# Making three rows' second products in one GpSimd instruction, in a buffer of its own, in a rotary-embedding kernel

## The chip, the cores and the metric

The kernel runs on one core of a Trainium2 chip. The metric is the device time of one execution in microseconds (us). Before the change it was 162.52 us, the median of 3 runs (162.47 to 162.65). A profile of one execution accompanies each kernel; its span, from the first instruction to the last, is 1.8 to 2.0 us shorter than the time.

## The reference

```python
batch, seq, dim = (16, 512, 1024); num_heads = 16      # head_dim 64, half_dim 32, all float32
x = x.reshape(batch, seq, num_heads, head_dim)
x1, x2 = x[..., :half_dim], x[..., half_dim:]
cos, sin = cos[None, :, None, :], sin[None, :, None, :]
out = concatenate([x1 * cos - x2 * sin, x1 * sin + x2 * cos], axis=-1)
```

Each element is one product with a cosine, one product of its partner in the other half of the head with a signed sine, and a sum. 32 MB are read and 32 MB written.

## The kernel before

The data go through in eight tiles of 4 MB. A tile has 128 partitions with 8 rows of 1024 elements each. GpSimd makes the second (sine) products of rows 1 to 7 into buffers `b`. VectorE (DVE) makes the cosine products into PSUM, the memory into which TensorE also adds. For the pairs (1, 2), (4, 5) and (6, 7) DVE also makes the sum. Row 3 goes half by half through one PSUM bank, `pe_ps`: DVE puts the cosine product there, TensorE adds `b` to it (a matmul with the identity), and ScalarE copies it out. Row 0 does without GpSimd.

```python
PAIRS = ((1, 2), (4, 5), (6, 7))
bp = ctx.enter_context(tc.tile_pool(name="bp", bufs=3))     # three buffers of 8 KB per partition
...
def sin_rows(t, k, n):                                     # GpSimd: n rows from row k
    b = bp.tile([P, 2 * dim], FP32, name="b")[:, : n * dim]
    sin_product(b, rows(t, k, n), k, n)
    return b
def pe_half(k, r, b):
    cos_product(pe_ps, r, k)                               # DVE
    pe_add(pe_ps, b)                                       # TensorE
    nc.scalar.copy(out=r, in_=pe_ps)                       # ScalarE
...
for t in range(NT):
    first, second, third = PAIRS
    b1 = sin_rows(t, first[0], 2)
    p1 = pair_product(t, first[0])                         # DVE
    ...                                                    # row 0: DVE, TensorE, ScalarE
    b3 = sin_rows(t, ROW_PE, 1)
    b2 = sin_rows(t, second[0], 2)
    pair_sum(*p1, b1)                                      # DVE
    h0, h1 = zip(parts(rows(t, ROW_PE)), parts(b3))
    pe_half(ROW_PE, *h0)
    p2 = pair_product(t, second[0])
    b1 = sin_rows(t, third[0], 2)
    pair_sum(*p2, b2)
    pe_half(ROW_PE, *h1)
    p1 = pair_product(t, third[0])
    if t + 1 < NT:
        cos_product(own_ps, rows(t + 1, ROW_OWN), ROW_OWN)
    pair_sum(*p1, b1)
    stores(t)
```

## Time and profile before

| | before |
|---|---|
| time, median | 162.52 us |
| span of the profile | 160.7 us |
| busy: DVE, GpSimd, TensorE, ScalarE | 136.3, 127.2, 56.4, 18.1 us |
| last store: issued, landed | 148.15, 159.84 us |

### The profile page before, as it was taken

Reading aid. Unit: us, or ns where it says so; the run is one execution under the profiler, and the core shown is the slowest. Engines: PE = TensorE matmul, PEld = TensorE weight load, DVE = VectorE, ACT = ScalarE, POOL = GpSimd, SP = SyncE. Lnnn points to the kernel's source line nnn. Section 1 sums busy time; section 2 is a strip of 40 time slices with the busy share of each in tenths; the row PEclk is TensorE's granted clock in tenths of the full one; section 3 lists DMA queues with packets and bytes.
Section 4 is the critical chain, followed back from the end, with each engine's and each line's share of the span. In section 5 each row is a group of like instructions: output and inputs, shape, how many; then the busy total and the mean of one; then the engine's idle time right before and its main releaser. Section 6 shows DMA issues by size and latency. Waiting matters only on the chain.

```text
span 160.7 us, 443 instructions
## 1 busy us (share of the span) xinstructions
PE 56.4 (35%) x71; PEld 18.8 (12%) x71; DVE 136.3 (85%) x85; ACT 18.1 (11%) x25; POOL 127.2 (79%) x38
## 2 busy tenths in 40 slices
PE   3131905064503731191309150745046402822000
PEld 0111301021102210121004010211021101210000
DVE  1059969999999999999999999999999999998000
ACT  0001311003000301021100310031003010201000
POOL 1049999999999999988998899898999899840000
PEclk9999985559555865567555855595558655675555
DMA  5999999999999999999999999999999999999993
GB/s 180 407 408 473 392 498 416 392 457 457 392 416 481 408 400 498 408 392 506 410 392 473 432 400 449 457 400 416 489 392 408 498 400 408 481 416 400 392 514 139
DMA packets 2619, 67.25 MB, mean 419 GB/s; under 512 B 314, under 2 KB 442, under 8 KB 442
## 3 DMA queue, kind: packets, MB, share of 16 engines
q1 hardware_dynamic: 2618, 67.24, 97.9%
q14 instruction: 1, 0.01, 0.0%
HBM read 33.69 MB, written 33.55 MB: 418 GB/s over the span
## 4 chain that ended last, share of the span: by engine, by line
DVE 68%; issue 12%; POOL 6%; DMA 4%; PE 1%; SPq 0%; DVEq 0%
DVE xt L189 33%; DVE pd L141 31%; POOL b L165 6%; DMA b<-in_sin_dram 4%; DVE pe_ps L141 3%; PE tab L113 1%; PE tab L114 1%; DVE sns L116 0%; DVE xt L150 0%; DVE own_ps L141 0%; SPq L74 0%; DVE sns L117 0%; DVEq L189 0%
## 5 line engine op out<-in xcount | busy, mean ns | idle before, releaser
L165 POOL TENSOR_TENSOR b<-xt,sns 128x2048 f32<-128x2048 f32 (+1 forms) x32 | 126.5, 3987 | 14.5 <-DVE sns L117 9.1
L189 DVE TENSOR_TENSOR xt<-pd,b 128x2048 f32<-128x2048 f32 x24 | 54.9, 2287 | 2.4 <-POOL b L165 1.6
L141 DVE TENSOR_TENSOR pd<-xt,tab 128x2048 f32<-128x2048 f32 x24 | 55.0, 2291 | 0.2
L176 PE MATMUL own_ps<-xt,ident 128*128 128x512 f32 x32 | 29.1, 1064 | 54.0 <-DVE xt L150 48.3
L176 PE MATMUL pe_ps<-b,ident 128*128 128x512 f32 x32 | 25.2, 880 | 29.1 <-DVE pe_ps L141 29.1
L176 PEld LDWEIGHTS own_ps<-xt,ident 128*128 128x128 f32 x32 | 9.4, 324 | 74.0 <-DVE xt L150 59.3
L209 ACT COPY xt<-own_ps 128x1024 f32<-128x1024 f32 x8 | 8.1, 1013 | 72.2 <-PE own_ps L176 72.2
L181 ACT COPY xt<-pe_ps 128x512 f32<-128x512 f32 x16 | 9.4, 589 | 40.7 <-PE pe_ps L176 40.7
L176 PEld LDWEIGHTS pe_ps<-b,ident 128*128 128x128 f32 x32 | 8.0, 279 | 43.8 <-DVE pe_ps L141 36.0
L141 DVE TENSOR_TENSOR pe_ps<-xt,tab 128x512 f32<-128x512 f32 x16 | 11.0, 686 | 0.0
L141 DVE TENSOR_TENSOR own_ps<-xt,tab 128x1024 f32<-128x1024 f32 x8 | 9.8, 1223 | 0.0
L150 DVE TENSOR_TENSOR xt<-xt,tab 128x1024 f32<-128x1024 f32 x8 | 9.7, 1214 | 0.0
L116 DVE TENSOR_SCALAR sns<-tab 128x256 f32<-128x256 f32 x1 | 0.4, 426 | 8.0 <-PE tab L114 8.0
L209 ACT ACT_TABLE_LOAD x1 | 1.3, 1283 | 15.3 <-DVE xt L150 15.3
L113 PE MATMUL tab<-b,spread 64*128 64x256 f32 x2 | 1.2, 697 | 4.9 <-DMA b<-in_sin_dram 4.9
L101 PE MATMUL own_ps<-zero 128*128 128x512 bf16 x2 | 1.0, 622 | 1.2 <-DVE zero L97 1.2
L113 PEld LDWEIGHTS tab<-b,spread 64*128 64x128 f32 x2 | 0.5, 308 | 5.7 <-issue 5.7
L114 PE MATMUL tab<-b,spread 64*128 64x256 f32 x2 | 1.1, 631 | 0.0
L97 DVE MEMSET zero<- 128x256 uint32 x1 | 0.3, 272 | 0.9 <-PEq L240 0.9
L114 PEld LDWEIGHTS tab<-b,spread 64*128 64x128 f32 x2 | 0.7, 333 | 0.2
L101 PE MATMUL pe_ps<-zero 128*128 128x512 bf16 x1 | 0.6, 634 | 0.0
L101 PEld LDWEIGHTS <-zero 128*128 128x128 bf16 x3 | 0.3, 125 | 1.5 <-DVE zero L97 1.2
(9 smaller groups left out, 1.8 us busy)
## 6 DMA issues: line engine op xcount, KB each, us to landing
out_dram<-xt SPq DMA_DIRECT2D x8, 4096.0 KB, 21.4
xt<-in_x_dram SPq DMA_DIRECT2D x7, 4096.0 KB, 38.8
xt<-in_x_dram SPq DMA_DIRECT2D x1, 2560.0 KB
xt<-in_x_dram SPq DMA_DIRECT2D x1, 1536.0 KB
spare<-in_sin_dram SPq DMA_DIRECT2D x5, 0.1 KB
b<-in_sin_dram SPq DMA_DIRECT2D x1, 64.0 KB
b<-in_cos_dram SPq DMA_DIRECT2D x1, 64.0 KB
```

The lines of the kernel that those rows point to most:

```text
L97: nc.vector.memset(zero, 0.0)
L101: nc.tensor.matmul(out=ps, lhsT=zero[:, :P], rhs=zero, start=True, stop=True)
L113: nc.tensor.matmul(out=sin_t, lhsT=spread, rhs=sin_sb, start=True, stop=True)
L114: nc.tensor.matmul(out=cos_t, lhsT=spread, rhs=cos_sb, start=True, stop=True)
L116: nc.vector.tensor_scalar_mul(out=sns[:, :, 0, :], in0=sin_k, scalar1=-1.0)
L141: nc.vector.tensor_tensor(out=o, in0=i, in1=cb, op=ALU.mult)
L150: nc.vector.tensor_tensor(out=heads(r), in0=heads(r), in1=s, op=ALU.mult)
L165: nc.gpsimd.tensor_tensor(out=o, in0=i, in1=sb, op=ALU.mult)
L176: nc.tensor.matmul(out=ps, lhsT=ident, rhs=other, start=False, stop=True, skip_group_check=True)
L181: nc.scalar.copy(out=r, in_=pe_ps)
L189: nc.vector.tensor_tensor(out=r, in0=ps, in1=b, op=ALU.add)
L209: nc.scalar.copy(out=r0, in_=own_ps)
```

## The change

The intent is fewer GpSimd instructions: rows 3, 4 and 5 lie side by side, so their second products can be one instruction. Its result needs 12 KB per partition. One of three 8 KB buffers is given up for it, and two small early tiles, `zero` and `spread`, are laid into the new buffer; together that frees 9.5 of the 12 KB. Seven no-ops are put on GpSimd ahead of its first wait.

```diff
+GROUPS = ((1, 2), (3, 3), (6, 2))
-    bp = ctx.enter_context(tc.tile_pool(name="bp", bufs=3))
+    bp = ctx.enter_context(tc.tile_pool(name="bp", bufs=2))
+    bp3 = ctx.enter_context(tc.tile_pool(name="bp3", bufs=1))
...
-    zero = fixed.tile([P, BANK], BF16)
+    for _ in range(7):
+        nc.gpsimd.nop(hint="pause")
+    early = bp3.tile([P, 3 * dim], FP32, name="b3")
+    zero = early[:, : BANK // 2].bitcast(BF16)
-    spread = fixed.tile([PB, P], FP32)
+    spread = early[:PB, BANK : BANK + P]
...
-        b3 = sin_rows(t, ROW_PE, 1)
-        b2 = sin_rows(t, second[0], 2)
+        b2 = sin_rows(t, *GROUPS[1])
         pair_sum(*p1, b1)
-        h0, h1 = zip(parts(rows(t, ROW_PE)), parts(b3))
+        h0, h1 = zip(parts(rows(t, ROW_PE)), parts(b2[:, :dim]))
...
-        pair_sum(*p2, b2)
+        pair_sum(*p2, b2[:, dim:])
```

More of the change, by code (lines that the diff above doesn't have):

```diff
@@ L167, in sin_rows @@
     def sin_rows(t, k, n):
-        b = bp.tile([P, 2 * dim], FP32, name="b")[:, : n * dim]
+        b = bp.tile([P, 2 * dim], FP32, name="b") if n == 2 else bp3.tile([P, 3 * dim], FP32, name="b3")
         sin_product(b, rows(t, k, n), k, n)
@@ L202 @@
         first, second, third = PAIRS
-        b1 = sin_rows(t, first[0], 2)
+        b1 = sin_rows(t, *GROUPS[0])
         p1 = pair_product(t, first[0])
@@ L209 @@
         nc.scalar.copy(out=r0, in_=own_ps)
-        b3 = sin_rows(t, ROW_PE, 1)
-        b2 = sin_rows(t, second[0], 2)
+        b2 = sin_rows(t, *GROUPS[1])
         pair_sum(*p1, b1)
-        h0, h1 = zip(parts(rows(t, ROW_PE)), parts(b3))
+        h0, h1 = zip(parts(rows(t, ROW_PE)), parts(b2[:, :dim]))
         pe_half(ROW_PE, *h0)
         p2 = pair_product(t, second[0])
-        b1 = sin_rows(t, third[0], 2)
-        pair_sum(*p2, b2)
+        b1 = sin_rows(t, *GROUPS[2])
+        pair_sum(*p2, b2[:, dim:])
         pe_half(ROW_PE, *h1)
```

## The prediction

> **What bounds the kernel now.** I read the page first: its busy shares, then the DMA row, then the chain that ended last.
>
> ```profile
> PE 56.4 (35%) x71; PEld 18.8 (12%) x71; DVE 136.3 (85%) x85; ACT 18.1 (11%) x25; POOL 127.2 (79%) x38
> DMA  5999999999999999999999999999999999999993
> q1 hardware_dynamic: 2618, 67.24, 97.9%
> HBM read 33.69 MB, written 33.55 MB: 418 GB/s over the span
> ```
>
> Two things are nearly full at once. The DMA queue moves 67.24 MB and its packets fill 97.9% of 16 engines' span of 160.7 us. VectorE is busy for 85% of the span, but between the first tile and the last it doesn't stop: cut into stretches of one tile (16.98 us), the view by windows shows this.
>
> ```profile
> 64.95:81.93 16.98, 6.50 (x8) 2.15 (x8) 16.84 (x11) 2.09 (x3) 15.84 (x5) 0.60 1.00 433
> 81.93:98.91 16.98, 6.55 (x8) 2.15 (x8) 16.84 (x11) 2.09 (x3) 15.85 (x5) 0.60 1.00 432
> ```
>
> The pairs are busy us and count for PE, PEld, DVE, ACT, POOL, then PEclk, DMA share and GB/s. DVE fills 16.84 of 16.98 us, GpSimd only 15.84; the DMA share is 1.00. So in the steady state DVE sets the pace of the computing, GpSimd has 1.14 us to spare per tile, and the transfers run through without a hole.
>
> The groups and the waits say where an instruction of GpSimd ever holds up DVE:
>
> ```profile
> L165 POOL TENSOR_TENSOR b<-xt,sns 128x2048 f32<-128x2048 f32 x24 | 108.4, 4530 | 14.5 <-DVE sns L117 9.1 <-DVE xt L189 5.4
> L165 POOL TENSOR_TENSOR b<-xt,sns 128x1024 f32<-128x1024 f32 x8 | 18.9, 2360 | 0.0
> L189 DVE TENSOR_TENSOR xt<-pd,b 128x2048 f32<-128x2048 f32 x24 | 54.9, 2287 | 2.4 <-POOL b L165 1.6
> ```
>
> DVE's sums (L189) lose 1.6 us to GpSimd in the whole run, in one wait: the timeline has it in tile 0 at 21.78 us, where the second pair's product is late because GpSimd could not start before 10.44 us. After tile 2 it is the other way round: GpSimd waits for DVE's sums to free a buffer (5.4 us, ten times).
>
> What ends the run is the last store. The trace has it issued at 148.15 us, right after DVE's last sum (145.80 + 2.29 = 148.09), and landed at 159.84. Whether it starts on idle or still busy DMA engines is seen in narrow windows around it (only the DMA columns count here):
>
> ```profile
> 148.55:148.95 0.40, 0.00 (x0) 0.00 (x0) 0.00 (x0) 0.00 (x0) 0.00 (x0) 0.50 0.20 82
> 148.95:149.35 0.40, 0.00 (x0) 0.00 (x0) 0.00 (x0) 0.00 (x0) 0.00 (x0) 0.50 2.87 1229
> 149.35:149.75 0.40, 0.00 (x0) 0.00 (x0) 0.00 (x0) 0.00 (x0) 0.00 (x0) 0.50 0.00 0
> 149.75:150.15 0.40, 0.00 (x0) 0.00 (x0) 0.00 (x0) 0.00 (x0) 0.00 (x0) 0.50 0.19 82
> 158.00:158.50 0.50, 0.00 (x0) 0.00 (x0) 0.00 (x0) 0.00 (x0) 0.00 (x0) 0.50 0.15 66
> 158.50:159.60 1.10, 0.00 (x0) 0.00 (x0) 0.00 (x0) 0.00 (x0) 0.00 (x0) 0.50 0.01 0
> ```
>
> Bytes count where a packet starts, and a packet has 32 KB. 82 GB/s over 0.40 us is one packet; 1229 is fifteen. So fifteen engines begin the last store at 148.95 to 149.35, some 0.8 us after its issue, while one engine started a packet of the store before at 148.6 (its packets take 1.2 us) and begins the last store only at 149.8. In the packets' own records the fifteen end at 158.7 to 159.0 and that one at 159.51. It never idles. **The end is thus the late DMA engine's, and DVE's last sum has a slack of about 159.51 - 159.0 = 0.5 us in front of it.**
>
> **What the Trainium skill says.** (1) "SBUF — State Buffer", Who interferes with whom: a DVE instruction with two SBUF inputs contends with a GpSimd instruction that reads SBUF, one with a single SBUF input doesn't. All the large DVE instructions here take one input from PSUM, and the trace agrees: the sum takes 2.29 us beside GpSimd and also at 145.80, when GpSimd is through. So a longer GpSimd instruction slows DVE by nothing. (2) "GPSIMD Engine Reference", Elementwise, side by side: 4497 ns for a tensor_tensor of 2048 f32; the trace has 4530. (3) "PSUM — Partial Sum Buffer", Engine vs sequencer instructions: a nop is executed by the sequencer alone, not by the datapath. The kernel before has none, so no row shows a cost. (4) "DMA: Bandwidth & Descriptors", Why a DMA increments its semaphore by 16: the 16 engines finish independently and only the full count means landed. That is the late engine above.
>
> **The change part by part.**
> *Products.* Per tile GpSimd made 2 rows + 1 row + 2 rows + 2 rows; now 2 + 3 + 2. From the two groups a row costs 4530 - 2360 = 2170 ns and an instruction 2360 - 2170 = 190 ns beside. A 3-row product is estimated at 190 + 3 x 2170 = 6.70 us, against 2.36 + 4.53 = 6.89. But the trace starts the next instruction some 0.05 us before the last ends (14.91 + 2.36 = 17.27, next start 17.22), so the gain is about 0.15 us per tile, 1.2 us over 8 tiles, of GpSimd's time. GpSimd is off the path after tile 0, so there it is worth nothing.
>
> *Tile 0, the second pair.* Before: 14.91 start of row 3, end of rows 4 and 5 near 21.74, sum at 21.78. After: 14.91 + 6.70 = 21.61, sum at about 21.64. DVE gains 0.14 us.
>
> *Tile 0, row 3.* Row 3's product was ready at 17.27; now it comes with the rest at 21.61. TensorE adds it into pe_ps, ScalarE copies it out, and only then can DVE put the second half's cos product into pe_ps. Before, TensorE's addition ran at 18.85 for 1.44 us and ScalarE's copy ended at 20.91, long before DVE came by at 23.99. Now: 21.65 + 1.44 (or 2.08, the same work at half clock at 24.73) + 0.06 + 0.59 + 0.03 = 23.8 to 24.4. DVE's sum would let it go on at 21.64 + 2.21 = 23.85. So DVE goes on at 23.85 to 24.4 instead of 23.99: a shift between **-0.14 and +0.45 us**, middle +0.15. The wait on b moves, partly, to a wait on ScalarE. As DVE has no hole after it, this shift is carried unchanged to the last sum.
>
> *Buffers.* Counting from the start of the second sum of a tile: the sum ends at 2.29, the second half's cos product at 2.9, TensorE's last reading of the 12 KB buffer at about 2.9 + 2.1 = 5.0. From there GpSimd makes the next 3-row product by 5.0 + 6.7 = 11.7. DVE fills its first half of pe_ps at 14.6 - 0.6 = 14.0 and takes the second sum at 16.98. So at the fastest GpSimd is 2.3 us ahead even of row 3's need and 5.3 ahead of the sum. The third pair follows by 16.2 (needed at 6.14 + 16.98 = 23.1), the next tile's first by 20.7 (needed at 28.8); then GpSimd waits until 22.0, which is some 1.3 us per tile of a wait in place of the two of 0.47 and 0.67 us it has now. No DVE wait. In tile 1, where GpSimd isn't ahead yet, the 3-row product ends at 21.6 + 2 x 4.47 + 6.7 = 37.2 (now the second pair's ends near 37.5); TensorE and ScalarE are through by 37.2 + 2.1 + 0.7 = 40.0, DVE comes at 40.96. Free by 0.9 us.
>
> *No-ops and the early tiles.* The seven no-ops come before GpSimd's wait of 9.1 us for the tables: they would have to cost 1.2 us each to show. zero and spread in the 12 KB buffer save 1.5 KB so that 28 KB of buffers fit in place of 24; their readers are through at about 10 us, well before the 3-row product at 14.91. Nothing.
>
> *Sum.* The last store is issued at 148.15 + (-0.14 to +0.45); its fifteen engines end at 159.0 + the same, up to 159.45, below the late engine's 159.51. Expected: 0.0 to 0.1 us. **162.6 us.**
>
> **The rivals.** *A: the shift comes through.* If the late engine is less late in the new kernel (its lag was not planned, as far as the page shows), the time follows DVE: between -0.5 (no late engine, shift -0.14) and +0.45. For: one engine out of 16 late by 0.5 us is a small thing. Against: before's three times agree within 0.18 us. 162.0 to 163.0. *B: the single 12 KB buffer becomes the bound.* A chain of sum, cos product, TensorE, product through one buffer: 11.7 us against a period of 16.98. It would need TensorE to come 2.3 us later than the throttled 2.08 us; then 8 tiles at some tenths: 163 to 165. Against it the spare time above. *C: GpSimd becomes the bound*, if a product over three rows costs more per element than over two; it would need 15.84 + 1.14: the 3-row product at over 7.9 us instead of 6.70. 1024 and 2048 elements lie on one straight line with a small intercept, which speaks against. *D: a gain*: the 1.57 us of DVE's wait in tile 0 doesn't go away, because all five rows are still made before the second sum; and anything gained there is stopped by 67.24 MB in the DMA queue.
>
> **Range and chances.** The middle is before plus 0.1; rival A gives -0.5 to +0.45, with the spread of runs of 0.2: 162.0 to 163.2 for 8 in 10. 2% is 3.25 us; the gain isn't there to be had (the DMA is full), the loss needs B or C. Faster 0.01, same 0.97, slower 0.02.
>
> **What would show it.** Right: 3-row products at 6.7 us, eight; DVE's wait on b in tile 0 near 1.4 us, with a wait of 0 to 0.5 us on ScalarE's copy after it; GpSimd's waits once a tile, on TensorE; period 16.98; last store issued at 148.0 to 148.6, landing near 159.8. Wrong: DVE waits on b or on ScalarE in several tiles, a period above 17.0, a 3-row product over 7 us, or a hole in the DMA row.

## The result, and the profile after

The changed kernel took 162.52 us, the median of 4 runs (162.47 to 162.64), beside 162.50 us for before. The ratio is 1.0004 with a 95% interval of 0.9987 to 1.0021: the same. (A ratio is the mean time of one kernel's fast runs over that of the other's of the same rounds, so it isn't quite the ratio of the medians quoted.) All runs were fast: none was over 1.5% above the fastest of its kernel.

| | before | after |
|---|---|---|
| time, median | 162.52 us | 162.52 us |
| GpSimd products, first start | 32, 10.44 us | 24, 10.70 us |
| GpSimd busy | 127.2 us | 125.7 us |
| last store: issued, landed | 148.15, 159.84 us | 148.83, 159.91 us |

The total stood still, but not all below it did. First four lines of the view of the groups with shapes kept apart, for the changed kernel (busy us, mean ns, then idle time before and its cause):

```profile
L171 POOL TENSOR_TENSOR b<-xt,sns 128x2048 f32<-128x2048 f32 x16 | 72.2, 4531 | 11.9 <-DVE sns L123 9.4 <-DMA xt<-in_x_dram 2.5
L195 DVE TENSOR_TENSOR xt<-pd,b 128x2048 f32<-128x2048 f32 x24 | 54.9, 2287 | 2.3 <-POOL b L171 1.4
L171 POOL TENSOR_TENSOR b<-xt,sns 128x3072 f32<-128x3072 f32 x8 | 53.5, 6693 | 2.4 <-PE pe_ps L182 2.4
L147 DVE TENSOR_TENSOR pe_ps<-xt,tab 128x512 f32<-128x512 f32 x16 | 11.0, 687 | 0.5 <-ACT xt L187 0.5
```

The three-row product takes 6.69 us. DVE's wait for GpSimd shrank from 1.6 to 1.4 us, and a new one of 0.5 us stands on row 3's cosine product, for ScalarE. GpSimd now waits for TensorE, which reads the 12 KB buffer last.

Where the new wait is, is seen in the timeline of tile 0. First before (start, duration, engine and line; the idle time of the engine before it in brackets):

```profile
18.85 1.44 PE L176 MATMUL pe_ps<-b,ident 128*128 128x512 f32 x2
...
20.32 0.59 ACT L181 COPY xt<-pe_ps 128x512 f32<-128x512 f32 x1 [0.22 <-PE pe_ps L176]
21.78 2.29 DVE L189 TENSOR_TENSOR xt<-pd,b 128x2048 f32<-128x2048 f32 x1 [1.57 <-POOL b L165]
...
23.99 0.69 DVE L141 TENSOR_TENSOR pe_ps<-xt,tab 128x512 f32<-128x512 f32 x1
```

Then after:

```profile
21.90 2.29 DVE L195 TENSOR_TENSOR xt<-pd,b 128x2048 f32<-128x2048 f32 x1 [1.44 <-POOL b L171]
...
21.92 2.07 PE L182 MATMUL pe_ps<-b,ident 128*128 128x512 f32 x2 [2.61 <-POOL b L171]
24.03 0.59 ACT L187 COPY xt<-pe_ps 128x512 f32<-128x512 f32 x1 [3.67 <-PE pe_ps L182]
24.65 0.70 DVE L147 TENSOR_TENSOR pe_ps<-xt,tab 128x512 f32<-128x512 f32 x1 [0.46 <-ACT xt L187]
```

Row 3's product is no longer ready at about 17 us but comes with rows 4 and 5 at 21.9 us. TensorE, ScalarE and DVE then follow one another. DVE goes on at 24.65 instead of 23.99 us, and since it waits for nothing afterwards (the period is 16.98 us as before), the last store is issued 0.68 us later. Of this, 0.26 us was there already when GpSimd began.

Yet the store landed only 0.07 us later. Three windows around the last store of the changed kernel (the last two columns are the DMA share and GB/s, counted where a packet starts):

```profile
148.95:149.35 0.40, 0.00 (x0) 0.00 (x0) 0.00 (x0) 0.00 (x0) 0.00 (x0) 0.50 0.01 0
149.35:149.60 0.25, 0.00 (x0) 0.00 (x0) 0.00 (x0) 0.00 (x0) 0.00 (x0) 0.50 0.00 0
149.60:150.00 0.40, 0.00 (x0) 0.00 (x0) 0.00 (x0) 0.00 (x0) 0.00 (x0) 0.50 3.05 1311
```

1311 GB/s over 0.40 us is sixteen packets of 32 KB: all sixteen engines begin the last store together, where before fifteen began at 149 us and the late one at 149.8. The later issue fell into time in which the late engine was still at work on the store before.

### The profile page after: what moved, and what is told of

It reads as the page before. It is cut to its first block, busy times and chain, and to the rows that moved or that the text cites. A ratio compares the mean times of both kernels' runs of the same rounds, so it can differ in the third digit from the quotient of the medians.

```text
span 160.7 us, 443 instructions
## 1 busy us (share of the span) xinstructions
PE 57.6 (36%) x71; PEld 18.7 (12%) x71; DVE 136.4 (85%) x85; ACT 18.1 (11%) x25; POOL 125.7 (78%) x30
## 4 chain that ended last, share of the span: by engine, by line
DVE 55%; POOL 19%; issue 8%; PE 6%; DMA 4%; ACT 0%; SPq 0%; DVEq 0%; POOLq 0%
DVE xt L195 27%; DVE pd L147 22%; POOL b L171 19%; PE pe_ps L182 5%; DVE pe_ps L147 4%; DMA b<-in_sin_dram 4%; PE tab L119 1%; PE tab L120 1%; ACT xt L187 0%; DVE sns L122 0%; SPq L77 0%; DVE sns L123 0%; DVE xt L156 0%; DVE own_ps L147 0%; DVEq L195 0%
## 5 line engine op out<-in xcount | busy, mean ns | idle before, releaser
L171 POOL TENSOR_TENSOR b<-xt,sns 128x2048 f32<-128x2048 f32 (+1 forms) x24 | 125.0, 5252 | 14.3 <-DVE sns L123 9.4
L182 PE MATMUL pe_ps<-b,ident 128*128 128x512 f32 x32 | 25.9, 904 | 28.3 <-DVE pe_ps L147 25.7
L119 PE MATMUL tab<-b,b 64*128 64x256 f32 x2 | 1.2, 696 | 5.1 <-DMA b<-in_sin_dram 5.1
L107 PE MATMUL own_ps<-b 128*128 128x512 bf16 x2 | 1.0, 622 | 1.2 <-DVE b L103 1.2
L119 PEld LDWEIGHTS tab<-b,b 64*128 64x128 f32 x2 | 0.5, 307 | 6.0 <-issue 6.0
L120 PE MATMUL tab<-b,b 64*128 64x256 f32 x2 | 1.1, 631 | 0.0
L120 PEld LDWEIGHTS tab<-b,b 64*128 64x128 f32 x2 | 0.7, 333 | 0.2
L107 PE MATMUL pe_ps<-b 128*128 128x512 bf16 x1 | 0.6, 634 | 0.0
```

The lines of the kernel that those rows point to most:

```text
L107: nc.tensor.matmul(out=ps, lhsT=zero[:, :P], rhs=zero, start=True, stop=True)
L119: nc.tensor.matmul(out=sin_t, lhsT=spread, rhs=sin_sb, start=True, stop=True)
L120: nc.tensor.matmul(out=cos_t, lhsT=spread, rhs=cos_sb, start=True, stop=True)
L171: nc.gpsimd.tensor_tensor(out=o, in0=i, in1=sb, op=ALU.mult)
L182: nc.tensor.matmul(out=ps, lhsT=ident, rhs=other, start=False, stop=True, skip_group_check=True)
```

## The experiments

Names beginning with `b_` are built on before, those with `a_` on the changed kernel. The "issue" is the start of the last store, "landing" the landing of it, both from the profiled execution. To make differences visible that the slack hides, the five kernels with `d22` in their names make one cosine product of a pair twice in tile 2. This changes no value and moved DVE's next tile 2.3 us later. b_d11 doubles a product of half that size. Every kernel gave correct results.

| kernel | first product | issue | landing | landing - issue | time, median (before beside it) |
|---|---|---|---|---|---|
| before | 10.44 | 148.15 | 159.84 | 11.69 | 162.52 |
| after | 10.70 | 148.83 | 159.91 | 11.08 | 162.52 (162.50) |
| a_again | 10.83 | 148.39 | 160.34 | 11.95 | 162.64 (162.46) |
| b_lead | 10.91 | 147.39 | 160.18 | 12.79 | 162.57 (162.37) |
| a_nonop | 10.55 | 148.12 | 159.82 | 11.70 | 162.50 (162.37) |
| b_d11 | 10.65 | 149.62 | 160.71 | 11.09 | 163.25 (162.37) |
| b_d22 | 10.39 | 150.45 | 161.54 | 11.09 | 164.22 (162.46) |
| a_t0_d22 | 10.45 | 150.49 | 161.57 | 11.08 | 164.56 (162.46) |
| a_d22 | 10.79 | 151.23 | 162.31 | 11.08 | 164.46 (162.46) |
| a_d22b | 10.42 | 150.85 | 161.92 | 11.07 | 164.59 (162.36) |
| a_fill_d22 | 10.39 | 150.29 | 161.37 | 11.08 | 164.08 (162.36) |
| b_2buf | 11.27 | 168.56 | 179.63 | 11.07 | 181.72 (162.37) |

### How much slack the last store has: b_d22 and b_d11

```diff
 # b_d22
         p1 = pair_product(t, third[0])
+        if t == 2:
+            cos_product(p1[0], p1[1], third[0], 2)
 # b_d11
             cos_product(own_ps, rows(t + 1, ROW_OWN), ROW_OWN)
+            if t == 2:
+                cos_product(own_ps, rows(t + 1, ROW_OWN), ROW_OWN)
```

> Before, with one cos product of 128x2048 made twice in tile 2: DVE loses 2.2 us in the steady state. Theory 1 (slack of about 0.6 us, then the time follows the last store's issue one for one: issue + 13.7 us): issue at 150.4, time 164.0 to 164.2, so 1.5 to 1.7 us more than before, not 2.2. Rival (the DMA queue alone is the bound, with much slack): time within 0.3 us of before. Rival (DVE alone is the bound): 2.2 us more.

> Before, with one cos product of 128x1024 made twice in tile 2: DVE loses 1.13 us. Theory 1 (slack about 0.6 us): issue near 149.3, time 0.4 to 0.6 us over before. Rival (DMA bound with wide slack): no more than 0.1 us over. Rival (DVE bound): 1.1 us over.

b_d22 took 164.22 us (164.13 to 164.29), a ratio of 1.0108 (1.0093 to 1.0122). That is 1.76 us more than before: neither nothing nor all of the delay. b_d11 took 163.25 us, ratio 1.0055 (1.0042 to 1.0067), 0.88 us more, which is above the 0.4 to 0.6 expected. The doubled product moved DVE by 1.27 us in the profile, not 1.13, and in the profiled run GpSimd had also begun 0.21 us later. Its issue was therefore 1.47 us later than before's and its landing 0.87. How late the other four runs began isn't recorded, and their times (163.15 to 163.34) are much the same, so some 0.2 us of the 0.88 stays unexplained.

The table's fifth column says the same without any reckoning. A last store that finds the DMA engines idle lands 11.07 to 11.09 us after its issue, in eight profiles (in after's the late engine came free just in time). Before's took 11.69 us. So **its slack was 11.69 - 11.08 = 0.61 us** in this profile, and after's was zero. The times agree roughly: 2.3 - 1.76 = 0.5 us from b_d22, 1.27 - 0.88 = 0.4 from b_d11.

### Does an earlier DVE gain anything: b_lead

In tile 0, rows 4 and 5 come before row 3 on GpSimd, and DVE does row 3's second half after the third pair's cosine product.

```diff
-        b3 = sin_rows(t, ROW_PE, 1)
-        b2 = sin_rows(t, second[0], 2)
+        if t == 0:
+            b2 = sin_rows(t, second[0], 2)
+            b3 = sin_rows(t, ROW_PE, 1)
+        else:
+            b3 = sin_rows(t, ROW_PE, 1)
+            b2 = sin_rows(t, second[0], 2)
...
-        pe_half(ROW_PE, *h1)
+        if t > 0:
+            pe_half(ROW_PE, *h1)
         p1 = pair_product(t, third[0])
+        if t == 0:
+            pe_half(ROW_PE, *h1)
```

> Before, with tile 0 in another order: rows 4 and 5 before row 3 on GpSimd, and on DVE row 3's second half after the third pair's cos product. DVE's wait of 1.6 us in tile 0 goes, the last store is issued 1.0 to 1.6 us earlier, at 146.5 to 147.2. Theory 1 (the DMA engines are full until 149 us and one is late): time unchanged, or up to 0.5 us less if the late engine is less late. Rival (DVE is the bound): 1.0 to 1.6 us less, 161.0 to 161.5.

It took 162.57 us, ratio 1.0014 (1.0002 to 1.0027): nothing gained. The view of the waits of DVE shows the wait for GpSimd almost gone, 0.2 us in place of 1.6:

```profile
DVE xt L189 <- POOL b L165: 0.2, 1, 0.2
```

The last store was issued at 147.39 us although this execution had begun 0.47 us late, and it landed 12.79 us after its issue, at 160.18. The DMA engines were not free earlier. So the kernel before stands on the DMA queue, and DVE may be later by 0.6 us or, as here, earlier by 0.76 + 0.47 = 1.2 us without the time changing.

### The no-ops: a_nonop

```diff
-    for _ in range(7):
-        nc.gpsimd.nop(hint="pause")
```

> The changed kernel without the seven no-ops. Theory: they lie in GpSimd's 9 us of waiting for the tables and take some 0.04 us each, so nothing changes: time within 0.15 us of the changed kernel and of before, GpSimd's first product at 10.4 to 10.7 us. Rival (they steer the fetch of instructions or the late DMA engine): the instruction packet at about 80 us moves or goes, or the time moves by 0.3 us or more.

162.50 us, ratio to before 1.0007 (0.9994 to 1.0021), and the first product at 10.55 us. The one instruction packet in mid-run stays where it was, at 79.8 us. In the changed kernel's trace the seven no-ops have 13 ns each and start 40 ns apart, from 0.98 to 1.22 us; GpSimd is then through with its set-up at 1.3 us and waits until 10.70. They do nothing that these runs show. What they were put in for stays open.

### Is the later issue the change's doing: a_again, a_d22 and a_t0_d22

a_again is the changed kernel once more, a_d22 the changed kernel with the doubled product. a_t0_d22 has, in tile 0 alone, the products apart again:

```diff
+        if t == 0:
+            b2 = bp3.tile([P, 3 * dim], FP32, name="b3")
+            sin_product(b2[:, :dim], rows(t, ROW_PE), ROW_PE, 1)
+            sin_product(b2[:, dim:], rows(t, second[0], 2), second[0], 2)
+        else:
+            b2 = sin_rows(t, *GROUPS[1])
```

> The changed kernel once more, beside before on the same chip. Theory 1 (the change costs DVE about 0.4 us in tile 0, a wait for ScalarE's copy, and the slack in front of the last store swallows it): time within 0.15 us of before, last store issued 0.4 us later than before's, and later still by what the tables happen to land later; DVE's wait for ScalarE 0.4 to 0.5 us, once. Theory 2 (the 0.68 us by which the last store came later was chance in the start alone): the issue varies and the wait for ScalarE is not there in this profile.

> The changed kernel with the same doubled product in tile 2. Theory 1: its slack is used up, so nearly the whole 2.2 us comes through: issue at 150.8 to 151.05, time 164.4 to 164.75, which is 0.4 us more than before with the same delay. Rival (the change shifts DVE by nothing; the later issue was chance): the same time as before with the delay, within 0.15 us.

> The changed kernel with the doubled product in tile 2, and in tile 0 alone the products of row 3 and of rows 4 and 5 made apart again, into the same 12 KB buffer. Theory 1 (what the change costs is the late product of row 3 in tile 0 and nothing else): no wait of DVE for ScalarE, time equal to before with the delay within 0.15 us, 0.4 us under the changed kernel with the delay. Rival (the single buffer or the longer product costs DVE something in later tiles too): it stays at or near the changed kernel's time.

None of the three came out as plainly as expected. a_again took 162.64 us, ratio 1.0012 (0.9998 to 1.0026): the same, but its profile has **no wait for ScalarE**, against my theory 1, and the store was issued only 0.24 us later than before's, less than the 0.39 us by which its first product was late. a_d22 took 164.46 us, inside the expected range, but by luck: its six times fall into two heaps, 164.94, 164.70, 164.82 and 164.06, 163.96, 164.22, with the median between them. Its issue, 151.23 us, lies above the expected range; GpSimd had begun at 10.79. a_t0_d22 took 164.56 us, 0.34 us above b_d22 and no better than a_d22: by the time alone the rival, a cost in later tiles, would have won. The profile speaks against it: no wait for ScalarE, issue 150.49 and landing 161.57 us against b_d22's 150.45 and 161.54. About half of the difference lies outside the span: the time is 1.9 to 2.0 us longer than the span, b_d22's 1.8. I have no cause for that.

The table settles what DVE loses if the start is taken out, that is, if the first product is subtracted from the issue. b_d22 has 140.06, a_t0_d22 140.04, a_d22 140.44 us. So in these profiles the later tiles, with one 12 KB buffer and three-row products, cost DVE nothing; tile 0 cost it 0.4 us in a_d22.

The two heaps go with the mean granted clock, TensorE's clock as a share of full speed. The slow three have 0.69, the fast three 0.642 to 0.645. That seems upside down, as a higher clock should not be slower, so I looked at TensorE in tile 0. In a_again (clock 0.646):

```profile
15.69 3.75 PE L182 MATMUL own_ps<-xt,ident 128*128 128x512 f32 x4 [5.74 <-POOL b L171]
22.04 1.12 PE L182 MATMUL pe_ps<-b,ident 128*128 128x512 f32 x2 [2.60 <-POOL b L171]
```

In the first profile of the changed kernel (0.691) the second of these lines reads 2.07 us. The same two matmuls ran at double speed in a_again. The rows of the clock on the two pages, first a_again's:

```profile
PEclk9999985559555865567555855595558555775555
```

and after's:

```profile
PEclk9999999999555775558555955585557755585555
```

The nines at the left are not a measurement of full speed: in both kernels row 0's four matmuls, at 15.6 us, take 3.75 us, the slow rate. The trace's first record of a clock is a raise to full speed: at 19.8 us in a_again and at 37.5 us in after. What stands before the first record is filled with nines. An execution that misses the early raise thus gets a *higher* mean on paper while its row 3 is added at half speed.

The reason suggested itself. Before, row 3's addition followed row 0's at once: in before's timeline TensorE goes from 15.30 to 20.29 us without a pause, 5 us. The change makes row 3 late, so TensorE works for 3.75 us, stands for 2.6 us, and whether the clock is raised in time is left to chance. "TensorE: Matmul & The Clock Gate", Part 1, says that the clock is raised after about 3.4 us of sustained work, judged in a window of 3.41 us that runs freely and doesn't start with the kernel, so that the moment differs from run to run. That would explain both heaps.

The traces can settle this. Their clock records last 3.41 us or a multiple of it (but for the last one), so the steps can be counted back into tile 0. For each step one can ask how much of it matmuls cover, by their records, whose ends are modelled. In the twelve profiles all 93 steps that end in a raise are covered to 79% or more, and the 333 others at the low clock to 71% or less. Row 0's 3.75 us can fill one step or be cut by its border. Before row 3 came, they covered a step to 90% in a_again, 79% in a_nonop and 86% in b_lead, which got the early raise. In after, a_d22 and a_d22b it was at most 66, 60 and 71%, and there was none. So the chance lies in where the steps fall when the kernel starts.

All 31 timed executions of before in these three calls have clocks of 0.641 to 0.652; of 27 of the changed kernel and its variants with a late row 3 (after, a_again, a_d22, a_nonop, a_d22b), 13 have 0.69. b_lead, where row 3 is late too, has two of five.

### Is it the clock: a_d22b and a_fill_d22

a_d22b is a_d22 unchanged. a_fill_d22 fills the gap on TensorE in tile 0:

```diff
+    zfill = fixed.tile([P, BANK], BF16)
+    nc.vector.memset(zfill, 0.0)
...
-    def pe_half(k, r, b):
+    def pe_half(k, r, b, fill=0):
         cos_product(pe_ps, r, k)
+        for _ in range(fill):
+            nc.tensor.matmul(out=pe_ps, lhsT=zfill[:, :P], rhs=zfill, start=False, stop=True, skip_group_check=True)
...
-        pe_half(ROW_PE, *h0)
+        pe_half(ROW_PE, *h0, fill=5 if t == 0 else 0)
```

> The changed kernel with the doubled product again. Theory 3, formed from the first eight runs: the wait for ScalarE in tile 0 comes only in executions in which TensorE isn't raised to full clock before row 3's addition (two matmuls in 2.07 us instead of 1.12); these have a mean granted clock of 0.69 by the profile, the others of 0.64 to 0.65. Executions of both kinds, those of 0.69 slower by 0.6 to 0.8 us: 164.0 to 164.2 against 164.7 to 164.9. Rival (chance of the DMA queue): no relation between the two kinds and the time.

> The changed kernel with the doubled product, and with five matmuls of zeros added into pe_ps in tile 0 (they change no value) in the 2.6 us in which TensorE otherwise stands between row 0's addition and row 3's. Theory 3 (the addition of row 3 used to follow row 0's at once and kept TensorE busy 5 us; the change tears the two apart, and the clock is raised or not by chance): with the gap filled, every execution has a mean clock of 0.64 to 0.66 and a time of 164.0 to 164.3, no wait for ScalarE. Rival (the gap has nothing to do with it): executions of 0.69 as before, or all at 164.7 to 164.9.

With the gap filled, all six executions have a clock of 0.648 to 0.657 and times of 163.98 to 164.25 us (median 164.08). Without, three of six have 0.69, and the times run from 164.15 to 165.03. The two profiles are a clean pair, as GpSimd began at 10.42 and 10.39 us and a step of the clock's record ends at 20.04 and at 20.05 us. In this step TensorE is busy for 2.41 us (71%, no raise) without the fill and for all of it with the fill, and the raise comes. The timeline of tile 0 in a_d22b:

```profile
21.63 2.07 PE L182 MATMUL pe_ps<-b,ident 128*128 128x512 f32 x2 [2.59 <-POOL b L171]
...
24.36 0.69 DVE L147 TENSOR_TENSOR pe_ps<-xt,tab 128x512 f32<-128x512 f32 x1 [0.46 <-ACT xt L187]
```

and in a_fill_d22, where the five small matmuls at 18.80 precede it:

```profile
18.80 1.86 PE L189 MATMUL pe_ps<-zfill 128*128 128x512 bf16 x5
...
21.62 1.13 PE L184 MATMUL pe_ps<-b,ident 128*128 128x512 f32 x2 [0.95 <-POOL b L173]
...
23.80 0.69 DVE L149 TENSOR_TENSOR pe_ps<-xt,tab 128x512 f32<-128x512 f32 x1
```

DVE goes on 0.56 us earlier, the last store is issued 0.56 us earlier (150.29 against 150.85) and lands 0.55 us earlier. Over the two runs of a_d22, the six executions at 0.69 average 164.78 us and the six at 0.64 average 164.24, or 164.14 without one of 164.77 that has no mark of its own; before has such an outlier too (163.65). In a_d22b alone only one of six times (164.15) lies in the band expected for its kind, and the kinds overlap. So the relation is not perfect execution by execution, but filling the gap removed the slow heap from six executions, and the size agrees.

In the changed kernel itself, without the doubled product, the slack swallows this: a_nonop's executions at 0.69 took 162.53, 162.42 and 162.50 us, those at 0.65 took 162.43 and 162.51.

### The buffers alone: b_2buf

```diff
-    bp = ctx.enter_context(tc.tile_pool(name="bp", bufs=3))
+    bp = ctx.enter_context(tc.tile_pool(name="bp", bufs=2))
```

> Before with its four products a tile, with two 8 KB buffers in place of three. Theory: the second pair's product then waits for the first sum (1.7 us of DVE a tile) and the third pair's for TensorE's last addition of row 3 (3.3 us a tile), so about 5 us a tile and 195 to 203 us in all; in the changed kernel it is the separate 12 KB buffer that keeps these two waits off DVE, not the merging as such. Rival (two buffers are enough, GpSimd is far from the bound): 162.5 to 165.

181.72 us, ratio 1.1198 (1.1175 to 1.1221). Two 8 KB buffers without the third or the 12 KB one cost 19 us, so the buffers matter; but I had expected 195 to 203. The timeline shows DVE's two waits of tile 2:

```profile
61.84 2.29 DVE L189 TENSOR_TENSOR xt<-pd,b 128x2048 f32<-128x2048 f32 x1 [1.83 <-POOL b L165]
...
68.75 2.29 DVE L189 TENSOR_TENSOR xt<-pd,b 128x2048 f32<-128x2048 f32 x1 [0.69 <-POOL b L165]
```

The first was expected at 1.7 us. The second is 0.69 and not 3.3 us: the third pair's product starts at 64.21 us, when the second sum ends, and not after TensorE's last addition of row 3 (66.86). It got the second pair's buffer, and I had assumed row 3's. In all DVE waits 21.3 us for GpSimd, in 16 waits, where before's waits 1.6. With the 0.83 us by which GpSimd began later that makes 20.5 us, and the issue did move by 20.4.

## Why the prediction was right

The time (162.6 predicted, 162.52 measured) and the main steps held.

- **What ends the run.** The late DMA engine with a slack of about 0.5 us was right; b_d22, b_d11 and b_lead show it, and the landing times give 0.61 us.
- **The products.** 6.70 us was predicted for three rows and 6.69 measured. DVE's wait for GpSimd in tile 0 was predicted near 1.4 us and is 1.44. Rival C falls with this.
- **Row 3 in tile 0.** The chain and the range of the shift (-0.14 to +0.45 us) were right; by the prediction's own figures the upper end is 24.41 - 23.99 = 0.42. What failed is its middle of +0.15: the profiles show no middle. Either the addition runs in 1.12 us and there is no wait, or in 2.07 us and DVE waits. The issue less the first product shows both ends: against before's 137.71 it is 137.56 in a_again and 137.57 in a_nonop (-0.15 and -0.14), and 138.13 in after (+0.42). The prediction took both durations from before's trace without asking what decides between them; a_fill_d22 and the steps of the clock show that it is whether TensorE's work fills a step or is torn apart.
- **The issue of the last store** was predicted at 148.0 to 148.6 and was 148.83 us. The term that was left out is the start: GpSimd's first product, which waits for the tables, began between 10.39 and 10.91 us, in kernels of both kinds (b_2buf aside). Here it cost 0.26 us. With that, the first profile of after used up the whole slack, 0.68 us against 0.61. That the landing still moved by only 0.07 us is in part luck; a later start would have shown in the time. This is not rival A, whose range was also worked out wrongly: without a late engine the end would be 159.0 us plus the shift, which is 0.1 to 0.65 us earlier than before, never later.
- **The buffers.** No DVE wait came of the single 12 KB buffer, so rival B falls. GpSimd's wait for TensorE was expected once a tile and came in three tiles, 2.4 us in all; one more of 2.5 us, not foreseen, was for a tile's load (`DMA xt<-in_x_dram` in the groups above). GpSimd gains about 1 us per tile on DVE and needs most of the run to get so far ahead.
- **The gain.** Eight instructions fewer on an engine with time to spare were worth nothing, as said, and b_lead shows that even 1.4 us less waiting on DVE is worth nothing here.

No experiment points to a version that beats both: b_lead made DVE 1.2 us earlier and ended at the same DMA queue.

## What to carry to other kernels

Take the time from issue to landing of the last store and subtract that of a like store that meets idle engines: the rest is the slack of all that leads up to its issue, and changes smaller than it can't be seen in the time. To test a small shift, first use the slack up, here with one doubled instruction. When merging instructions, ask who used the first part early; making that part late can also break up TensorE's work and, with it, take away its full clock.

## What the Trainium skill lacked or had wrong

- "TensorE: Matmul & The Clock Gate", Part 1, describes a raise after sustained work. The runs agree, and add a case at the edge: 5 us of matmuls in one piece got the early raise in 31 of 31 executions (by their mean clock), 3.75 us followed by a pause in about half (14 of 27). The page doesn't say how full a window must be; here 79% or more got the raise (93 of 93) and 71% or less didn't (333 of 333). It also has nothing on how a mean granted clock is to be read when the first record is a raise; here the executions with 0.69 were the ones that *missed* the early raise, with the addition at 2.07 instead of 1.12 us.
- "DMA: Bandwidth & Descriptors", Anatomy of one DMA, fits about 2 us fixed plus bytes at 436 GB/s, but for DMAs that GpSimd issues. It has no such fit for those that SyncE issues, as here. Taken over to the 4 MB store the fit would give 2 + 9.6 = 11.6 us, an estimate from the page; the runs show 11.07 to 11.09 us from issue to landing when the engines are idle. No page says that a longer figure can be used as a measure of slack.
- "PSUM — Partial Sum Buffer", Engine vs sequencer instructions, says that a nop belongs to the sequencer but gives no cost there. The trace has seven at 13 ns each, 40 ns apart.
